# A row-sum kernel: early first loads, a 126+2 row layout with a split store, and a last row in three pieces

## The chip, the cores and the metric

The kernel runs on one core of one Trainium2 chip. Its engines are DVE (VectorE), ACT (ScalarE), POOL (GpSimd), PE (TensorE, unused here) and SP (SyncE, which issues the DMA transfers of this kernel; SPq is its queue). A transfer is issued by SP, is carried out as packets by 16 DMA engines, and ends with 16 completions (semaphore increments); its landing is the last of these. The metric is the device time of one execution in microseconds (us). A kernel is run several times; the text quotes medians. Ratios are the mean time of one kernel's fast runs over that of the other's fast runs of the same rounds on the same chip, so they are not quite the ratio of the medians quoted. The profile's span is some 1.8 us shorter than the device time of the same execution (162.6 and 164.42 us for the kernel before). The profiled execution of the kernel before is 0.4 us above its median.

## The reference

```python
def setup_inputs():
    batch, seq, dim = 32, 512, 1024
    return {"x": np.random.randn(batch, seq, dim).astype(np.float32), "divisor": float(dim)}

def reference(x, divisor):
    return (np.sum(x, axis=-1) / divisor).astype(np.float32)
```

So 16,384 rows of 1024 float32 (67.1 MB) are read, and 16,384 results (64 KB) are written.

## The kernel before

Partition p of 128 gets the 128 consecutive rows from 128p on. The rows come in nine bulk loads (14 rows per partition, the last one 8), then loads of 4, 2 and 1 rows, then the last row in two pieces. DVE (`reduce_sum`) and ACT (an activation that also sums) share the rows of each load. All results stand in one tile `res` of 128 x 128, which one store writes at the end: 512 B per partition, 512 B apart.

```python
    xr = x.tensor.reshape((P, J, D)).ap()          # P = 128 partitions, J = 128 rows each, D = 1024
    out_v = out.tensor.reshape((P, J)).ap()
    bulk = [14] * 7 + [14, 8]; tail = [4, 2]
    # ... three buffers of 14 rows; sums() splits each load between ACT and DVE ...
    c = 704
    t = one.tile([P, D], F32, name="row")          # the row before the last: one load, two sums
    # ... ACT sums t[:, c:], DVE sums t[:, :c], DVE combines and scales; DVE scales res[:, :126] ...
    t = one.tile([P, D], F32, name="last")         # the last row: two loads
    tc.keep_in_program_order(nc.sync.dma_start(out=t[:, :c], in_=xr[:, j, :c]))
    tc.keep_in_program_order(nc.sync.dma_start(out=t[:, c:], in_=xr[:, j, c:]))
    act_sum(part[:, 2:3], t[:, :c])
    nc.vector.reduce_sum(out=part[:, 3:4], in_=t[:, c:], axis=AX)
    nc.vector.tensor_scalar(out=res[:, j : j + 1], in0=part[:, 3:4], scalar1=part[:, 2:3],
                            scalar2=scale, op0=ADD, op1=MULT)
    tc.keep_in_program_order(nc.sync.dma_start(out=out_v, in_=res))
```

## Time and profile before

| What | Value | Read from |
|---|---|---|
| device time | 163.96 us (163.89 to 164.11) | three runs |
| DVE, ACT busy | 49%, 38% of the span | the page, part 1 |
| one DMA packet of 57,344 B | 2.116 us, so 27.1 GB/s on one of 16 engines, 434 GB/s on all | the trace's packets |
| first load issued, first load packet | 0.73 us, 1.74 us | timeline, packets |
| last load packet ends, last load's completion | 158.90 us, 159.35 us | packets, completion increments |
| last store issued, completed, span's end | 160.22, 161.77, 162.6 us | timeline, completion increments |

The first lines of the page show that the loads are the bound: neither compute engine is half busy, while DMA is at nine tenths in nearly every slice.

```profile
span 162.6 us, 213 instructions
DVE 79.3 (49%) x16; ACT 61.1 (38%) x115; POOL 0.2 (0%) x4
DMA  6999999989999999899999999999999999998990
GB/s 226 451 451 451 451 437 395 437 353 409 451 451 451 451 451 437 381 423 395 423 423 451 451 453 451 451 451 437 409 409 423 409 423 423 443 435 383 423 373 22
```

What can be saved lies at the two ends. The waits of SP's queue (who waited, for whom, us in total, times, longest) show at one end the opening barrier and at the other the completion of the store:

```profile
SPq L108 <- PEq L108: 0.7, 1, 0.7
SPq L122 <- DMA out_dram<-res: 1.0, 1, 1.0
```

The timeline of the start and of the end (start us, duration us, engine, line, operation) and the line of the store in the DMA view (count, KB, us from issue to landing):

```profile
0.73 1.33 SPq L61 DMA_DIRECT2D t<-in_x_dram  x3
...
159.03 0.76 ACT L50 ACTIVATE junk<-last 128x704 f32<-128x704 f32 x1 [0.32 <-DMA last<-in_x_dram]
159.27 0.21 DVE L76 TENSOR_SCALAR res<-part 128x1 f32<-128x1 f32 x1
159.40 0.47 DVE L87 TENSOR_REDUCE part<-last 128x1 f32<-128x320 f32 x1
159.98 0.21 DVE L88 TENSOR_SCALAR res<-part 128x1 f32<-128x1 f32 x1
160.22 0.35 SPq L91 DMA_DIRECT2D out_dram<-res  x1
```

```profile
out_dram<-res SPq DMA_DIRECT2D x1, 64.0 KB, 1.5
```

From the last landing (159.35) to the issue of the store (160.22) it takes 0.87 us, and from there to the landing of the store 1.55 us.

### The profile page before, as it was taken

The page shows a single profiled execution, that of the slowest core. Times are in us where ns is not written, and L with a number is a line of the kernel's source. Part 1 is how long each engine was busy: PE and PEld are TensorE (multiplying, and loading weights), DVE is VectorE, ACT ScalarE, POOL GpSimd, SP SyncE. Part 2 cuts the span into 40 slices and gives each one's busy share as a digit, 9 for nine tenths or more (in the row PEclk, how much of TensorE's full clock was granted, in tenths as well). Part 3 has the DMA queues.
Part 4 walks back from the last instruction along what each step waited for, and adds up shares of the span by engine and source line. Part 5 has one row for each costly group of instructions (what it writes and reads, how often), then busy time and mean ns, then how long its engine had stood idle before and what let it go on. Part 6 is the DMA issues. An engine that isn't in the chain of part 4 may idle for free.

```text
span 162.6 us, 213 instructions
## 1 busy us (share of the span) xinstructions
DVE 79.3 (49%) x16; ACT 61.1 (38%) x115; POOL 0.2 (0%) x4
## 2 busy tenths in 40 slices
DVE  0000099207940596039801990099108930697893
ACT  3000096006800490029201940095007700692882
POOL 0000000000000000000000000000000000000000
DMA  6999999989999999899999999999999999998990
GB/s 226 451 451 451 451 437 395 437 353 409 451 451 451 451 451 437 381 423 395 423 423 451 451 453 451 451 451 437 409 409 423 409 423 423 443 435 383 423 373 22
DMA packets 2161, 67.18 MB, mean 413 GB/s; under 512 B 240, under 2 KB 496, under 8 KB 752
## 3 DMA queue, kind: packets, MB, share of 16 engines
q1 hardware_dynamic: 2160, 67.18, 96.5%
q14 instruction: 1, 0.01, 0.0%
HBM read 67.11 MB, written 0.07 MB: 413 GB/s over the span
## 4 chain that ended last, share of the span: by engine, by line
DMA 74%; DVE 18%; another core or an unknown queue 5%; SPq 1%; issue 0%; DVEq 0%
DMA t<-in_x_dram 48%; DMA tail<-in_x_dram 25%; DVE res L56 17%; DVE part L75 0%; SPq L61 0%; SPq L66 0%; DVE part L87 0%; DVE res L79 0%; DVE res L88 0%; DVE res L76 0%; DVEq L88 0%; DVEq L76 0%; DVEq L79 0%
## 5 line engine op out<-in xcount | busy, mean ns | idle before, releaser
L56 DVE TENSOR_REDUCE res<-t 128x8 f32<-128x8192 f32 (+1 forms) x9 | 73.9, 8212 | 79.9 <-DMA t<-in_x_dram 79.9
L50 ACT ACTIVATE junk<-t 128x1024 f32<-128x1024 f32 x52 | 52.5, 1009 | 96.7 <-DMA t<-in_x_dram 96.7
L50 ACT ACTIVATION_READ_ACCUMULATOR junk<-t 128x1 f32 x52 | 9.7, 186 | 0.0
L56 DVE TENSOR_REDUCE res<-tail 128x2 f32<-128x2048 f32 (+1 forms) x2 | 3.5, 1753 | 0.7 <-DMA tail<-in_x_dram 0.7
L50 ACT ACTIVATE junk<-tail 128x1024 f32<-128x1024 f32 x3 | 3.1, 1022 | 0.9 <-DMA tail<-in_x_dram 0.9
L50 ACT ACT_TABLE_LOAD x1 | 1.3, 1283 | 0.7 <-PEq L108 0.7
L50 ACT ACTIVATE junk<-last 128x704 f32<-128x704 f32 x1 | 0.8, 761 | 0.3 <-DMA last<-in_x_dram 0.3
L75 DVE TENSOR_REDUCE part<-row 128x1 f32<-128x704 f32 x1 | 0.9, 880 | 0.0
L50 ACT ACTIVATION_READ_ACCUMULATOR junk<-tail 128x1 f32 x3 | 0.6, 186 | 0.0
L50 ACT ACTIVATE junk<-row 128x320 f32<-128x320 f32 x1 | 0.4, 441 | 0.1
L87 DVE TENSOR_REDUCE part<-last 128x1 f32<-128x320 f32 x1 | 0.5, 475 | 0.0
L79 DVE TENSOR_SCALAR res<-res 128x126 f32<-128x126 f32 x1 | 0.2, 228 | 0.1
L88 DVE TENSOR_SCALAR res<-part 128x1 f32<-128x1 f32 x1 | 0.2, 214 | 0.1
L76 DVE TENSOR_SCALAR res<-part 128x1 f32<-128x1 f32 x1 | 0.2, 214 | 0.1
L50 ACT ACTIVATION_READ_ACCUMULATOR junk<-last 128x1 f32 x1 | 0.2, 187 | 0.0
L50 ACT ACTIVATION_READ_ACCUMULATOR junk<-row 128x1 f32 x1 | 0.2, 186 | 0.0
L108 POOL MEMSET const-bfloat16-1.0<- 128x1 bf16 x1 | 0.1, 101 | 0.0
L108 POOL MEMSET const-uint8-127<- 128x1 uint8 x1 | 0.1, 101 | 0.0
L108 POOL MEMSET const-float32-0.0<- 128x1 f32 x1 | 0.1, 98 | 0.2 <-issue 0.2
L108 POOL MEMSET const-float32-1.0<- 128x1 f32 x1 | 0.1, 98 | 0.0
## 6 DMA issues: line engine op xcount, KB each, us to landing
t<-in_x_dram SPq DMA_DIRECT2D x8, 7168.0 KB, 42.1
t<-in_x_dram SPq DMA_DIRECT2D x1, 4096.0 KB, 34.8
tail<-in_x_dram SPq DMA_DIRECT2D x1, 2048.0 KB, 39.3
tail<-in_x_dram SPq DMA_DIRECT2D x1, 1024.0 KB, 41.4
row<-in_x_dram SPq DMA_DIRECT2D x1, 512.0 KB, 42.2
last<-in_x_dram SPq DMA_DIRECT2D x1, 352.0 KB, 42.6
last<-in_x_dram SPq DMA_DIRECT2D x1, 160.0 KB, 42.5
out_dram<-res SPq DMA_DIRECT2D x1, 64.0 KB, 1.5
```

The costliest lines, as they stand in the source:

```text
L50: nc.scalar.activation(junk[:, :n], src, COPY, accum_out=dst)
L56: nc.vector.reduce_sum(out=res[:, j : j + d], in_=t[:, :d, :], axis=AX)
L75: nc.vector.reduce_sum(out=part[:, 1:2], in_=t[:, :c], axis=AX)
L76: nc.vector.tensor_scalar(out=res[:, j : j + 1], in0=part[:, 1:2], scalar1=part[:, 0:1], scalar2=scale, op0=ADD, op1=MULT)
L79: nc.vector.tensor_scalar_mul(out=res[:, :j], in0=res[:, :j], scalar1=scale)
L87: nc.vector.reduce_sum(out=part[:, 3:4], in_=t[:, c:], axis=AX)
L88: nc.vector.tensor_scalar(out=res[:, j : j + 1], in0=part[:, 3:4], scalar1=part[:, 2:3], scalar2=scale, op0=ADD, op1=MULT)
L108: nc = _bacc.Bacc("TRN2", target_bir_lowering=False, num_devices=1)
```

## The change

Three things change at once. (1) The first three loads, which wait for nothing, move ahead of the program's opening barrier. (2) The rows are laid out in two regions: partition p takes 126 consecutive rows of the first 16,128 rows, and 2 consecutive rows of the last 256. The 126 results per partition can leave early in a store of their own, and the last store carries only 8 B per partition (1 KB in all, side by side in memory). (3) The last row comes in three pieces, and the scaling moves partly to POOL and ACT.

```diff
+def start_loads_at_once(nc):
+    sp = mybir.EngineType.SP
+    first, body = nc.main_func.blocks[0], nc.main_func.blocks[1]
+    # ... SP's leading DMAs without a wait are taken out of `body` ...
+    first.instructions = first.instructions[:at] + loads + first.instructions[at:]   # ahead of SP's drain
 ...
+    nc.at_finalize(start_loads_at_once)
-    xr = x.tensor.reshape((P, J, D)).ap()
-    out_v = out.tensor.reshape((P, J)).ap()
+    L = 2
+    M = J - L
+    x_main = bass.AP(tensor=x.tensor, offset=0, ap=[[M * D, P], [D, M], [1, D]])
+    x_last = bass.AP(tensor=x.tensor, offset=P * M * D, ap=[[L * D, P], [D, L], [1, D]])
+    o_main = bass.AP(tensor=out.tensor, offset=0, ap=[[M, P], [1, M]])
+    o_last = bass.AP(tensor=out.tensor, offset=P * M, ap=[[L, P], [1, L]])
 ...
-    # last row: load [:704], load [704:], ACT and DVE sum, DVE combines, one store of res
+    c = 768
+    act_sum(r[:, 0:1], row[:, c:], by=scale)
+    nc.vector.reduce_sum(out=q[:, 0:1], in_=row[:, :c], axis=AX)
+    a, b = 512, 768
+    load(pa, x_last[:, 1, :a])
+    load(pb, x_last[:, 1, a:b])
+    load(pc[:, : D - b], x_last[:, 1, b:])
+    nc.gpsimd.tensor_scalar_mul(out=res, in0=res, scalar1=scale)
+    tc.keep_in_program_order(nc.sync.dma_start(out=o_main, in_=res))
+    act_sum(pc[:, D - b : D - b + 1], pa)
+    nc.vector.reduce_sum(out=pc[:, D - b + 1 :], in_=pb, axis=AX)
+    nc.vector.reduce_sum(out=q[:, 1:2], in_=pc, axis=AX)
+    nc.vector.scalar_tensor_tensor(out=fin, in0=q, scalar=scale, in1=r, op0=MULT, op1=ADD)
+    tc.keep_in_program_order(nc.sync.dma_start(out=o_last, in_=fin))
```

More of the change, by code (lines that the diff above doesn't have):

```diff
@@ L12 @@
 AX = mybir.AxisListType.X
+def start_loads_at_once(nc):
+    sp = mybir.EngineType.SP
+    first, body = nc.main_func.blocks[0], nc.main_func.blocks[1]
+    loads = []
+    for i in body.instructions:
+        if i.engine == sp:
+            if type(i).__name__ != "InstDMACopy" or (i.sync_info and i.sync_info.on_wait):
+                break
+            loads.append(i)
+    names = {i.name for i in loads}
+    assert names
+    body.instructions = [i for i in body.instructions if i.name not in names]
+    at = next(
+        k for k, i in enumerate(first.instructions) if i.engine == sp and type(i).__name__ == "InstDrain"
+    )
+    first.instructions = first.instructions[:at] + loads + first.instructions[at:]
 @with_exitstack
@@ L29 @@
     assert J * P == N
-    xr = x.tensor.reshape((P, J, D)).ap()
-    out_v = out.tensor.reshape((P, J)).ap()
-    bulk = [14] * 7 + [14, 8]
+    L = 2
[4 more added lines that the diff above has]
+    o_last = bass.AP(tensor=out.tensor, offset=P * M, ap=[[L, P], [1, L]])
     split = {14: 6, 8: 4, 4: 2, 2: 1}
-    tail = [4, 2]
@@ L39 @@
-    assert sum(bulk) + sum(tail) + 2 == J
-    pool = ctx.enter_context(tc.tile_pool(name="bulk", bufs=3))
+    loads = [14] * 8 + [8, 4, 2]
+    assert sum(loads) == M
+    bulk = ctx.enter_context(tc.tile_pool(name="bulk", bufs=3))
     one = ctx.enter_context(tc.tile_pool(name="one", bufs=1))
     psum = ctx.enter_context(tc.tile_pool(name="junk", bufs=4, space=bass.MemoryType.PSUM))
-    res = one.tile([P, J], F32, name="res")
-    part = one.tile([P, 4], F32, name="part")
-    def act_sum(dst, src):
+    res = one.tile([P, M], F32, name="res")
@@ L48, in act_sum, with load @@
+    fin = one.tile([P, L], F32, name="fin")
+    q = one.tile([P, L], F32, name="q")
+    r = one.tile([P, L], F32, name="r")
+    nc.gpsimd.memset(r, 0.0)
+    def load(dst, src):
+        tc.keep_in_program_order(nc.sync.dma_start(out=dst, in_=src))
+    def act_sum(dst, src, by=1.0):
         n = src.shape[-1]
         junk = psum.tile([P, D], F32, name="junk")
-        nc.scalar.activation(junk[:, :n], src, COPY, accum_out=dst)
-    def sums(t, j, rows):
+        nc.scalar.activation(junk[:, :n], src, COPY, scale=by, accum_out=dst)
@@ L53, in sums @@
+    j = 0
+    for rows in loads:
+        if rows >= 8:
+            t = bulk.tile([P, 14, D], F32, name="t")
+        else:
+            t = one.tile([P, rows, D], F32, name=f"t{rows}")
+        load(t[:, :rows, :], x_main[:, j : j + rows, :])
         d = rows - split[rows]
-        for r in range(d, rows):
-            act_sum(res[:, j + r : j + r + 1], t[:, r, :])
+        for i in range(d, rows):
+            act_sum(res[:, j + i : j + i + 1], t[:, i, :])
         nc.vector.reduce_sum(out=res[:, j : j + d], in_=t[:, :d, :], axis=AX)
-    j = 0
@@ L59 @@
-    for i, rows in enumerate(bulk):
-        t = pool.tile([P, 14, D], F32, name="t")
-        tc.keep_in_program_order(nc.sync.dma_start(out=t[:, :rows, :], in_=xr[:, j : j + rows, :]))
-        sums(t, j, rows)
-        j += rows
-    for i, rows in enumerate(tail):
-        t = one.tile([P, rows, D], F32, name=f"tail{i}")
-        tc.keep_in_program_order(nc.sync.dma_start(out=t, in_=xr[:, j : j + rows, :]))
-        sums(t, j, rows)
-        j += rows
-    c = 704
-    t = one.tile([P, D], F32, name="row")
@@ L73 @@
-    tc.keep_in_program_order(nc.sync.dma_start(out=t, in_=xr[:, j, :]))
-    act_sum(part[:, 0:1], t[:, c:])
-    nc.vector.reduce_sum(out=part[:, 1:2], in_=t[:, :c], axis=AX)
-    nc.vector.tensor_scalar(
-        out=res[:, j : j + 1], in0=part[:, 1:2], scalar1=part[:, 0:1], scalar2=scale, op0=ADD, op1=MULT
-    )
-    nc.vector.tensor_scalar_mul(out=res[:, :j], in0=res[:, :j], scalar1=scale)
-    j += 1
-    t = one.tile([P, D], F32, name="last")
-    tc.keep_in_program_order(nc.sync.dma_start(out=t[:, :c], in_=xr[:, j, :c]))
@@ L85 @@
-    tc.keep_in_program_order(nc.sync.dma_start(out=t[:, c:], in_=xr[:, j, c:]))
-    act_sum(part[:, 2:3], t[:, :c])
-    nc.vector.reduce_sum(out=part[:, 3:4], in_=t[:, c:], axis=AX)
-    nc.vector.tensor_scalar(
-        out=res[:, j : j + 1], in0=part[:, 3:4], scalar1=part[:, 2:3], scalar2=scale, op0=ADD, op1=MULT
-    )
-    tc.keep_in_program_order(nc.sync.dma_start(out=out_v, in_=res))
+        j += rows
+    c = 768
+    row = one.tile([P, D], F32, name="row")
+    load(row, x_last[:, 0, :])
@@ new lines @@
+    act_sum(r[:, 0:1], row[:, c:], by=scale)
+    nc.vector.reduce_sum(out=q[:, 0:1], in_=row[:, :c], axis=AX)
+    a, b = 512, 768
+    pa = one.tile([P, a], F32, name="pa")
+    pb = one.tile([P, b - a], F32, name="pb")
+    pc = one.tile([P, D - b + 2], F32, name="pc")
+    load(pa, x_last[:, 1, :a])
[3 more added lines that the diff above has]
+    tc.keep_in_program_order(nc.sync.dma_start(out=o_main, in_=res))
```

## The prediction

> **What bounds the kernel.** The loads. In the DMA view 67.11 MB are read; the 14-row packets (57,344 B) take 2.116 us each, 27.1 GB/s on one of 16 engines, 434 GB/s together. The Trainium skill ("DMA: Bandwidth & Descriptors", Specifications) gives 435 GB/s as the fabric ceiling; the trace agrees. The engines have no gaps: the first load packet starts 1.74 us after the span's start, the last ends at 158.90, and the packets at their median durations alone need 155.2 us. DVE (49%) and ACT (38%) mostly wait for loads. So only the two ends can give anything: the head (first issue at 0.73 us, first packet 1.0 us later) and the tail (from the last landing at 159.35 us to the end at 162.6).
>
> **Head.** The waits view shows SP waiting 0.7 us for the opening barrier. With the loads ahead of it, the first issue moves from 0.73 to about 0.05 us, and the saturated stream moves with it: -0.65 to -0.7 us, all on the critical path. The barrier then ends later (three issues of about 0.4 us), which delays ACT's table load to about 2 us; the first data come at 19 us, so that costs nothing.
>
> **Layout.** Per partition the bulk loads are the same runs of 56 KB; only the distance between partitions changes, from 512 to 504 KB. Since the packets already run at the ceiling, I expect no change of the rate (within 0.3 us either way; this is the part I know least).
>
> **Tail, after the shift of 0.7 us.** The last row in pieces of 512, 256 and 256 columns costs about 0.06 us more DMA time than 704 and 320 (128 more packets of some 8 ns overhead, from 1280 B = 55 ns and 2816 B = 113 ns). The last piece lands at about 158.75 us. DVE: row piece of 768 columns to 158.35, second piece 158.4 to 158.8 (256 columns, an estimate of 0.41 us from 704 = 0.88 and 320 = 0.475), last reduction (258 columns, 0.41 us) about 158.9 to 159.3, final operation 0.21 us plus 0.1 us, so the store is issued at about 159.65 instead of 160.22: -0.55 us. From last landing to issue it takes 0.9 us against 0.87 before, so this restructuring by itself is about neutral: it replaces ACT's 704 columns after the last but one landing by one more DVE step. The 126 columns leave early (POOL scaling, off the path; issue near 158), hidden behind the final computation.
>
> **Last store.** 64 KB in 512 B packets (27 ns each, 8 per engine) becomes 8 B per partition; packets of about 10 ns (the semaphore writes of 4 B take 9) would save 0.14 us. The skill says that below 512 B the DMA does read-modify-write (same section); no run here shows its cost, so I count -0.1 us with 0.4 us of risk. Issue to landing was 1.5 us and is mostly latency, which stays.
>
> **Sum.** -0.7 (head) + 0.06 (pieces) + 0.05 (chain) - 0.1 (store) = -0.7 us: 163.96 becomes 163.2 us, range 162.5 to 163.8. That is 0.4%, so within 2%.
>
> **Right or wrong, what shows it.** First DMA issue near 0 and first packet near 1.0 us (head); median 14-row packet still 2.116 us and 16.9 us between bulk reductions (layout); last landing about 158.7; DVE's last operation ends about 159.65; last store's issue to landing 1.4 to 1.5 us.
>
> **What would make it wrong.** The timed span starting with the issue, so that the head gains nothing; a slower first issue; the 504 KB stride changing HBM behaviour, for better (the first packets of each engine took 2.5 to 3.0 us) or worse; 8-byte writes with a slow receipt; the main store or POOL blocking SP's queue before the last store.

## The result, and the profile after

The changed kernel takes 165.05 us (164.85 to 165.28, four runs) against 164.04 us for the kernel before on the same chip: ratio 1.0061, 95% interval 1.0042 to 1.0079. It was forecast to be 0.7 to 0.8 us faster (163.2 against 163.96) and is 1.0 us slower.

The same lines of the changed kernel: the timeline of the start and of the end, then its stores in the DMA view, then the waits of SP's queue.

```profile
0.00 1.34 SPq L76 DMA_DIRECT2D t<-in_x_dram  x3
...
157.92 0.35 SPq L115 DMA_DIRECT2D out_dram<-res  x1
157.99 0.60 ACT L81 ACTIVATE junk<-pa 128x512 f32<-128x512 f32 x1
158.27 0.42 DVE L118 TENSOR_REDUCE pc<-pb 128x1 f32<-128x256 f32 x1
158.52 0.19 ACT L81 ACTIVATION_READ_ACCUMULATOR junk<-pa 128x1 f32 x1
158.79 0.42 DVE L119 TENSOR_REDUCE q<-pc 128x1 f32<-128x258 f32 x1
159.31 0.16 DVE L120 SCALAR_TENSOR_TENSOR fin<-q,r 128x2 f32<-128x2 f32 x1
159.50 0.34 SPq L121 DMA_DIRECT2D out_dram<-fin  x1
```

```profile
out_dram<-res SPq DMA_DIRECT2D x1, 63.0 KB, 2.1
out_dram<-fin SPq DMA_DIRECT2D x1, 1.0 KB, 2.8
```

```profile
SPq L138 <- PEq L138: 0.2, 1, 0.2
SPq L152 <- DMA out_dram<-fin: 2.4, 1, 2.4
```

Up to the issue of the last store, all went as forecast: the loads start at 0.00 us instead of 0.73, the last landing is at 158.59 us (159.35 before), and the last store is issued at 159.50 us, 0.72 us earlier than before. Then the store of 1 KB takes 2.84 us from issue to landing where the store of 64 KB took 1.55. The wait for it at the end of the program grew from 1.0 to 2.4 us. So the two traces put the loss in this one store: -0.72 us at its issue, +1.29 us in its flight and +0.05 us from its landing to the end of the span (0.88 us before, 0.93 after) are +0.6 us, the difference of the two spans (162.65 and 163.27).

Its packets show where in its flight. Before, the 512 B packets ended at 161.42 us, and the 16 completions came between 161.59 and 161.77. After, the 8 B packets ended at 160.54 us (each took 9 ns), and the completions came between 160.75 and 162.34, scattered over 1.6 us. By these records the data had left quickly; the time went between the last packet and the last completion.

### The profile page after: what moved, and what is told of

It is laid out like the page before. It is cut to its first block, busy times and chain, and to the rows that moved or that the text cites. A ratio compares the mean times of both kernels' runs of the same rounds, so it can differ in the third digit from the quotient of the medians.

```text
span 163.3 us, 220 instructions
## 1 busy us (share of the span) xinstructions
DVE 79.4 (49%) x15; ACT 60.9 (37%) x115; POOL 0.8 (1%) x6
## 4 chain that ended last, share of the span: by engine, by line
DMA 74%; DVE 17%; another core or an unknown queue 5%; SPq 2%; issue 0%; DVEq 0%
DMA t<-in_x_dram 48%; DMA pb<-in_x_dram 26%; DVE res L93 16%; SPq L76 2%; DVE q L119 0%; DVE pc L118 0%; DVE fin L120 0%; DVEq L119 0%; DVEq L120 0%
## 5 line engine op out<-in xcount | busy, mean ns | idle before, releaser
L93 DVE TENSOR_REDUCE res<-t 128x8 f32<-128x8192 f32 (+3 forms) x11 | 77.4, 7038 | 79.8 <-DMA t<-in_x_dram 79.8
L81 ACT ACTIVATE junk<-t 128x1024 f32<-128x1024 f32 x55 | 55.5, 1010 | 95.8 <-DMA t<-in_x_dram 95.8
L81 ACT ACTIVATION_READ_ACCUMULATOR junk<-t 128x1 f32 x55 | 10.3, 187 | 0.0
L114 POOL TENSOR_SCALAR res<-res 128x126 f32<-128x126 f32 x1 | 0.5, 535 | 155.5 <-DVE res L93 155.5
L101 DVE TENSOR_REDUCE q<-row 128x1 f32<-128x768 f32 x1 | 1.0, 953 | 0.1
L81 ACT ACTIVATE junk<-pa 128x512 f32<-128x512 f32 x1 | 0.6, 601 | 0.1
```

The lines of the kernel that those rows point to most:

```text
L81: nc.scalar.activation(junk[:, :n], src, COPY, scale=by, accum_out=dst)
L93: nc.vector.reduce_sum(out=res[:, j : j + d], in_=t[:, :d, :], axis=AX)
L101: nc.vector.reduce_sum(out=q[:, 0:1], in_=row[:, :c], axis=AX)
L114: nc.gpsimd.tensor_scalar_mul(out=res, in0=res, scalar1=scale)
```

## The experiments

### First round: which part of the change loses the time?

My theory was that the head gained what was forecast and that the last store lost more. Two explanations of the small store were open. Theory A: a write of less than 512 B is completed slowly, whatever its neighbours. Theory B: 128 small writes into the same 1 KB get in each other's way. Rivals of both: the early start, or the three pieces, disturb the end of the program. All four kernels ran on one chip in five rounds, with the kernel before at 164.19 us.

**hoist_only**: the kernel before, with `start_loads_at_once` and nothing else.

```diff
+    nc.at_finalize(start_loads_at_once)
```

> The kernel before with only the first three loads ahead of the opening barrier. My theory (the head gains what was predicted, the last store loses more): first issue near 0, first packet near 1.0 us, everything after it 0.65 to 0.75 us earlier, last store issue to landing 1.5 us as before, so about 0.7 us (0.4%) faster than the kernel before, near 163.3 us. Rival (the early start gains nothing in the timed span, or is lost later in the stream): the same time as before, 163.9 to 164.2 us.

Measured: 163.43 us, 0.76 us below the kernel before (ratio 0.9954, interval 0.9941 to 0.9968). First packet 1.00 us, last landing 158.33 us, and the store as before:

```profile
0.00 1.32 SPq L83 DMA_DIRECT2D t<-in_x_dram  x3
...
159.22 0.35 SPq L113 DMA_DIRECT2D out_dram<-res  x1
```

```profile
out_dram<-res SPq DMA_DIRECT2D x1, 64.0 KB, 1.5
```

The head of the prediction holds; the early start alone gives a better kernel than either of the two.

**no_hoist**: the changed kernel without that line.

```diff
-    nc.at_finalize(start_loads_at_once)
```

> The changed kernel with its loads behind the barrier again. If head and tail simply add up: about 0.7 us slower than the changed kernel, 165.7 us, with the last store still taking about 2.8 us from issue to landing. Rival (starting early is what disturbs the end of the program): the last store falls back to 1.5 us and the time to about 164.4 us.

Measured: 165.62 us (ratio 1.0089, interval 1.0076 to 1.0103); the last store still takes 2.75 us from issue to landing (the view rounds it to 2.7):

```profile
out_dram<-fin SPq DMA_DIRECT2D x1, 1.0 KB, 2.7
```

The early start does not cause the slow store. From the two ratios, the early start is worth 0.0028, or 0.5 us, in the changed kernel; the two ran in different rounds, and their intervals allow the 0.76 us seen above. In the two traces the last store is issued 0.70 us earlier with the early start (159.50 and 160.20).

**aligned_split**: the changed kernel with the 128-row layout. The two stores stay, but the 8 B per partition now go to places 512 B apart.

```diff
-    x_main = bass.AP(...); x_last = bass.AP(...); o_main = bass.AP(...); o_last = bass.AP(...)
+    xr = x.tensor.reshape((P, J, D)).ap()
+    out_v = out.tensor.reshape((P, J)).ap()
+    x_main, x_last = xr[:, :M, :], xr[:, M:, :]
+    o_main, o_last = out_v[:, :M], out_v[:, M:]
```

> The changed kernel with its 128-row layout back, but still two stores: the last one writes 8 bytes per partition, now 512 B apart and no longer side by side in 1 KB. Theory A (a write of under 512 B is completed slowly whatever its neighbours): the last store takes 2.4 to 3.2 us from issue to landing, time 164.7 to 165.4 us. Theory B (128 small writes into the same 1 KB get in each other's way): the last store takes 1.4 to 1.7 us, time 163.3 to 163.8 us.

Measured: 163.54 us (ratio 0.9961, interval 0.9948 to 0.9973). The same 8 B per partition now take 1.42 us:

```profile
out_dram<-res SPq DMA_DIRECT2D x1, 63.0 KB, 1.5
out_dram<-fin SPq DMA_DIRECT2D x1, 1.0 KB, 1.4
```

Theory A falls: pieces of 8 B are as small here as in the changed kernel.

**one_store**: the 128-row layout and one store of `res`, as before; early loads and three pieces kept.

```diff
-    nc.gpsimd.tensor_scalar_mul(out=res, in0=res, scalar1=scale)
-    tc.keep_in_program_order(nc.sync.dma_start(out=o_main, in_=res))
+    nc.gpsimd.tensor_scalar_mul(out=res[:, :M], in0=res[:, :M], scalar1=scale)
 ...
-    nc.vector.scalar_tensor_tensor(out=fin, in0=q, scalar=scale, in1=r, op0=MULT, op1=ADD)
-    tc.keep_in_program_order(nc.sync.dma_start(out=o_last, in_=fin))
+    nc.vector.scalar_tensor_tensor(out=res[:, M:], in0=q, scalar=scale, in1=r, op0=MULT, op1=ADD)
+    tc.keep_in_program_order(nc.sync.dma_start(out=out_v, in_=res))
```

> The changed kernel with the 128-row layout and a single last store of 512 B per partition; three last pieces and early loads kept. Both theories of the small store: it takes 1.5 us from issue to landing, and is issued near 159.5 us of the span as in the changed kernel, so 163.4 us, about 1.5 us faster than the changed kernel. Rival (the extra time comes from the three pieces or from the early start, not from the store): stays above 164.5 us.

Measured: 163.64 us (ratio 0.9969, interval 0.9956 to 0.9981), store issued at 159.48 us and landed 1.55 us later. So the three pieces are no loss of 1 us; beside hoist_only (163.43) they gain nothing either, and 0.2 us more is within the two intervals.

### Second round: is it the neighbourhood of the writes, and what in it?

aligned_split changed the layout of the loads, too. **packed_only** takes that away: it is aligned_split but for the destination of the last store. Its result is wrong.

```diff
-    o_main, o_last = out_v[:, :M], out_v[:, M:]
+    o_main = out_v[:, :M]
+    o_last = bass.AP(tensor=out.tensor, offset=P * M, ap=[[L, P], [1, L]])
```

> The 128-row layout of aligned_split for all loads and for the main store; only the last store's 128 pieces of 8 bytes go side by side into one 1 KB (so the result is wrong, on purpose). Theory B (neighbouring small writes get in each other's way): last store 2.4 to 3.1 us from issue to landing, about 1.3 us slower than aligned_split, near 164.9 us. Rival (the 126+2 layout of the loads, or the main store of 504 B runs, is what slows the end): 1.4 us and 163.5 us as aligned_split.

Measured: 165.06 us (ratio 1.0046, interval 1.0034 to 1.0059). In its trace:

```profile
out_dram<-res SPq DMA_DIRECT2D x1, 63.0 KB, 1.5
out_dram<-fin SPq DMA_DIRECT2D x1, 1.0 KB, 3.2
```

The two edits differ in the addresses of 128 writes and in nothing else, and the ratios (each against the kernel before on its own chip) differ by 0.0085, or 1.4 us. One thing comes with the addresses: the 1 KB lies inside what the main store writes, so here the last store also waits for the main store. That costs nothing: the main store landed at 159.25 us and DVE's last sum ended at 159.29. The changed kernel has no such overlap and is slow too. This settles the cause: the 8 B pieces side by side. The layout of the loads and the main store is not it.

**widths** adds 15 stores to the end of the kernel before, each issued after the landing of the one before it, with the pieces' width and spacing varied. A full store at the end makes the result right.

```diff
+    def again(name, w, step):
+        s = one.tile([P, w], F32, name=name)
+        nc.vector.tensor_copy(out=s, in_=res[:, :w])
+        to = bass.AP(tensor=out.tensor, offset=0, ap=[[step, P], [1, w]])
+        tc.keep_in_program_order(nc.sync.dma_start(out=to, in_=s))
+        nc.vector.memset(s, 0.0)
+    again("w2s2", 2, 2); again("w2s4", 2, 4)   # ... and so on; w and step in elements of 4 B
```

> The kernel before, then 15 further stores, one after the other, each on an idle queue: 8 bytes per partition at a spacing of 8, 16, 32, 64, 128, 256 and 512 bytes, then 64 B and 256 B side by side, 64 B at 512 B, 504 B side by side and at 512 B, and repeats of 8 B. Theory B: from issue to landing 2.5 to 3 us at a spacing of 8 B, falling to 1.4 us at a spacing that is the size of the shared block (64 B is my guess, so slow at 8, 16 and 32, fast from 64 or 128 on); 64 B and 256 B side by side fast; 504 B side by side somewhat slow (about 2 us, as pieces share blocks at their ends), 504 B at 512 B fast. Theory A (size alone) is already against aligned_split: it would make every store here but the 512 B one slow. The total time is not compared.

Measured, from issue to landing: 8 B at a spacing of 8 B took 2.83 us and on repetition 2.90 us; at 16, 32, 64, 128, 256 and 512 B it took 1.39 to 1.50 us. Pieces of 64 B and 256 B side by side took 1.41 and 1.44 us, and 504 B 1.55 us side by side and 1.52 at 512 B. The direction of theory B holds, but my guess that 16 B and 32 B would also be slow was a miss in this run.

**spacings** repeats part of this forwards and backwards with further patterns (`run16B`: pieces of 16 B side by side; `gap16B`: 8 B every 16 B; `eng4KB`: groups of eight 8 B pieces 32 B apart, the groups 4 KB apart; x marks the second pass). That each group falls to one DMA engine, as the expectations here and in the next run have it, is an assumption: the traces do not show which engine writes which piece. I forgot the full store at the end, so its result is wrong; the stores' times are not touched by that. Each store still waited for the one before.

```diff
+    again("gap8B", 2, [[2, P]], 0); again("run4B", 1, [[1, P]], 0)
+    again("eng4KB", 2, [[1024, 16], [8, 8]], 0)   # ... nine patterns, then the same backwards
```

> The kernel before, then 18 stores on an idle queue to a region written just before: nine patterns, then the same nine backwards. The width probe had 8 B at a spacing of 8 B slow (2.8 to 2.9 us) and 8 B at 16 B fast (1.4 us). If the spacing of 8 B is what is slow and order does not matter: gap8B 2.8 us in both passes, gap16B 1.4 us in both. If what counts is how many pieces fall into one block of 64 B: run4B slow as gap8B or slower, run16B and run32B (each piece beside the next, 4 and 2 to a block) 1.4 us. The eng patterns put an engine's eight 8 B pieces 32 B apart and vary the distance between engines: 4 KB was slow; if the distance matters, 512 B is near 1.4 us and the time grows towards 4 KB; if the form of the pattern (two steps) is what is slow, all four are alike.

Its DMA view (last column: us from issue to landing):

```profile
out_dram<-gap8B SPq DMA_DIRECT2D x1, 1.0 KB, 3.0
out_dram<-gap16B SPq DMA_DIRECT2D x1, 1.0 KB, 1.7
out_dram<-run4B SPq DMA_DIRECT2D x1, 0.5 KB, 7.4
out_dram<-run16B SPq DMA_DIRECT2D x1, 2.0 KB, 2.7
out_dram<-run32B SPq DMA_DIRECT2D x1, 4.0 KB, 1.4
...
out_dram<-eng4KB SPq DMA_DIRECT2D x1, 1.0 KB, 3.8
...
out_dram<-run32Bx SPq DMA_DIRECT2D x1, 4.0 KB, 1.4
out_dram<-run16Bx SPq DMA_DIRECT2D x1, 2.0 KB, 1.4
out_dram<-run4Bx SPq DMA_DIRECT2D x1, 0.5 KB, 7.5
out_dram<-gap16Bx SPq DMA_DIRECT2D x1, 1.0 KB, 2.5
out_dram<-gap8Bx SPq DMA_DIRECT2D x1, 1.0 KB, 3.1
```

For pieces that follow each other evenly, crowding goes with the time: 4 B side by side 7.4 and 7.5 us, 8 B 3.0 and 3.1 us, 32 B 1.4 us both times. At four pieces to 64 B the time varies between passes and runs: 1.4 or 2.7 us for 16 B side by side, 1.4 to 2.5 us for 8 B at 16 B. A second effect shows that crowding in 64 B is not the whole story: 8 B at a spacing of 32 B takes 1.4 us when it runs on evenly over 4 KB (the width probe), but with the groups 512 B, 1 KB, 2 KB and 4 KB apart 2.2, 1.8, 2.8 and 3.8 us in the first pass and 1.8, 2.5, 2.6 and 3.7 us in the second. These two-step patterns also start their packets some 0.4 us later (1.2 instead of 0.83 us after the issue), which leaves little to explain at 512 B and some 2 us at 4 KB. So the distance between groups matters, as one of the expectations had it, and the form of the pattern is not all. What in the memory makes the writes wait for each other stays open.

**who_shares** asked whether a block shared between engines or an engine's own successive writes cost more.

```diff
+    again("own64", 2, [[1024, 16], [2, 8]])   # groups of eight pieces side by side, groups 4 KB apart
+    again("mix64", 2, [[2, 16], [32, 8]])     # the 1 KB of pack2, its pieces in another order
```

> The kernel before, then eight further stores, one after the other: 8 bytes per partition 512 B apart (far2), side by side (pack2, twice), and with the neighbours chosen: own64 and own256 put the eight pieces of one DMA engine side by side (8 B or 32 B apart) with engines 4 KB apart; mix64 and mix256 put pieces of 16 different engines side by side and the pieces of one engine 128 B or 512 B apart. If a block shared between engines is what costs: mix slow (2 us or more), own fast (1.4 us). If one engine's successive writes to one block queue up: own slow, mix fast. If both: both slow.

Measured: far2 1.41, pack2 2.82 and 3.47, own64 3.95, mix64 3.13, own256 4.30, mix256 1.78 us. This does not decide between the two accounts. own256, whose groups are also 4 KB apart but less crowded, is as slow as own64, so the distance alone may make own64 slow. mix64 fills the same 1 KB as pack2 in another order and takes as long, and mix256 has the addresses of the fast 32 B spacing of widths and is fast but for its later start. What these runs show is that the set of addresses goes with the time in these two pairs, whatever the order.

**fresh** asked whether memory that this execution had not yet written is slower.

```diff
+    again("newgap8B", 2, [[2, P]], 0)      # ... first stores to unwritten parts, before any full store
+    again("newrun504B", 126, [[126, P]], 0)
+    again("oldrun504B", 126, [[126, P]], 0)
```

> The kernel before with its store replaced by 11 stores on an idle queue, the first to parts of the result that this execution has not written yet, the later ones to parts already written, and a full store at the end. The changed kernel's 504 B store took 2.1 us in its place and 1.5 us in the width probe, where the region had just been written. If memory not written yet is what is slow: newrun504B about 2 us or more, oldrun504B 1.5 us, newgap16B and newgap32B above 1.4 us, oldgap16B 1.4 us. If it makes no difference: 504 B 1.5 us both times, 8 B at a spacing of 8 B 2.8 us both times, 8 B at 16 B 1.4 us both times.

The run is inconclusive for its first five stores and for its last two of 8 B: they go to disjoint places, so they did not wait for each other and overlapped. The 504 B store took 1.66 us the first time and 2.16 us the second, the wrong way round for the idea of fresh memory. In all runs with it side by side it took between 1.5 and 2.4 us, and 512 B apart 1.5 us in every run; why it varies is open. In the changed kernel it lands at 159.98 us, before the last store's first packet at 160.34.

### Third: better versions

**fused_end** is aligned_split with the last reduction and scaling in one DVE operation.

```diff
-    act_sum(pc[:, D - b : D - b + 1], pa)
-    # ... reduce pb and pc, then scalar_tensor_tensor
+    act_sum(r[:, 1:2], pa, by=scale)
+    # ... DVE combines the row before the last, then reduces pb into pc[:, 256]
+    nc.vector.tensor_scalar(out=pd, in0=pc[:, : D - b + 1], scalar1=scale, scalar2=r[:, 1:2],
+                            op0=MULT, op1=ADD, accum_out=fin[:, 1:2])
```

> An attempt at a better kernel: aligned_split, with the last reduction and the final scaling in one DVE operation that starts its sum from ACT's scaled part. The final operation (0.16 us and 0.1 us before it) leaves the chain and a read of the accumulator comes in: last store issued 0.1 to 0.25 us earlier, 163.3 to 163.45 us against 163.54. If the fused operation is slower by more than it saves, no gain.

Measured: 163.42 us, ratio 0.9954 (0.9939 to 0.9968), not told apart from aligned_split (0.9961). From last landing (158.51) to issue (159.40) it takes 0.89 us, no less than in the kernel before: DVE was still busy with the pieces before.

**tuned_end** balances those pieces.

```diff
-    c = 768;  a, b = 512, 768
+    c = 640;  a, b = 512, 704
+    # and the combination of the row before the last runs on POOL
```

> fused_end with the ends of the two engines balanced: the row before the last is cut at 640 instead of 768 columns, the last row in 512, 192 and 320, and the combination for the row before the last runs on POOL, so that DVE is free when its pieces land. Last landing to issue of the last store about 0.65 to 0.75 us instead of 0.9, so 163.15 to 163.3 us, against 163.42 for fused_end and hoist_only. If the chain is not bound there, 163.4 us.

Measured: 163.29 us, ratio 0.9946 (0.9932 to 0.9959). Last landing 158.34, issue 159.12: 0.78 us instead of 0.89, not the 0.65 to 0.75 hoped for. The interval overlaps that of hoist_only.

**eight_rows** keeps the whole idea of the change, two regions and a last store side by side, but with 120+8 rows, so that the last store's pieces are 32 B.

```diff
-    L = 2
+    L = 8          # the loads of 4 and 2 rows now come from x_last, their sums go to fin
```

> The changed kernel with its idea kept (rows in two regions, split store, last store side by side) but 120+8 rows instead of 126+2, so that the last store's pieces are 32 B, two to each 64 B instead of eight. By the spacing probe (32 B side by side: 1.4 us in both passes; 8 B: 3.0 and 3.1 us) the last store takes 1.4 to 1.5 us from issue to landing and the kernel 163.4 to 163.7 us, like aligned_split. Rival (the layout of two regions, in loads or main store, has a cost of its own): above 164.2 us although the pieces are wider.

Measured: 163.22 us beside 164.05 us for the kernel before, ratio 0.9950 (0.9937 to 0.9963). That is faster than expected: its last load landed at 158.09 us, 0.5 us earlier than in the changed kernel, and no run isolates why. The main store waits behind the queued loads (5.1 us) and is complete before the last one is issued at 159.06 us; the last one is as fast as expected:

```profile
out_dram<-res SPq DMA_DIRECT2D x1, 60.0 KB, 5.1
out_dram<-fin SPq DMA_DIRECT2D x1, 4.0 KB, 1.4
```

A store four times as large takes half the time. All three of these, and hoist_only, beat the kernel before by some 0.5% (and the changed kernel by some 1%), and their intervals overlap; hoist_only gets it with the least code.

## Why the prediction was wrong

- **What bounds the kernel**: right. The packets' median is 2.116 us in both kernels, and the compute engines wait in both. The Trainium skill ("DMA: Bandwidth & Descriptors", Specifications) puts the fabric ceiling at 435 GB/s; the trace's packets make 434.
- **Head, -0.65 to -0.7 us**: right; hoist_only measured -0.76 us, and the first packet came at 1.02 us, as forecast.
- **Layout of the loads, no change of rate**: right. The packets' mean, which a median can hide, is 2.124 to 2.138 us in the traces with 128-row layout and 2.132 in those with two regions. The same skill page (Latency and other measured facts) reports copies between HBM tensors at a row pitch of 512 KiB at 207 GB/s, against 214 at a pitch of 4 MiB padded by 4 KiB. This kernel's loads show no such difference: 2.116 us per packet (median) at 512 KB and at 504 KB.
- **Tail, store issued at about 159.65 us and neutral by itself**: right to 0.15 us; it was issued at 159.50. From last landing to issue it took 0.91 us (0.9 forecast).
- **Last store, "I count -0.1 us with 0.4 us of risk"**: this is the step that failed. It measured +1.29 us in the trace, and 1.4 us in the comparison of packed_only with aligned_split. The term was mis-sized because I treated a small write as a matter of its width. The packets were indeed 9 ns each and ended early; the completions came late. Why such writes complete late stays open. The -0.1 us is what the same store gives 512 B apart (1.42 instead of 1.55 us). The skill's remark on read-modify-write below 512 B pointed at a cost, but the runs put it on the crowding of the pieces.
- Among what would make it wrong I had named "8-byte writes with a slow receipt", but gave it far too little weight: the range ended at 163.8 us.

The sum from the separate runs: -0.76 (head, hoist_only), +0.2 (three pieces, one_store against hoist_only), -0.1 (splitting the store, aligned_split against one_store), +1.4 (side by side, packed_only against aligned_split): +0.7 us. The two middle terms are not told apart from zero by their intervals. The measured ratio of 1.0061 is +1.0 us with an interval of 0.7 to 1.3 us.

## What to carry to other kernels

A store at the very end of a program is paid from issue to the last confirmation, so look at the landing of the last DMA and not at its bytes; a smaller last store can be slower. Where many partitions write to neighbouring places, try pieces of 32 B or more (32, 64 and 256 B took 1.4 us), or pieces evenly apart (8 B every 512 B was fast in each run); here that was worth 1.4 us. Distance alone is no guarantee: groups of 8 B pieces 4 KB apart were slow. Loads that wait for nothing can start ahead of the opening barrier, which gave this load-bound kernel the whole 0.7 us of that wait.

## What the Trainium skill lacked or had wrong

- "DMA: Bandwidth & Descriptors", Specifications: the line on transfers below 512 B gives a width for line rate and a read-modify-write below it, but nothing on how close the writes lie to each other. For the time of one store, width alone did not decide here: 8 B per partition took 1.42 us from issue to landing when 512 B apart and 2.7 to 3.2 us side by side in the kernels (up to 3.5 in a probe); 512 B took 1.55 us.
- No page that I read has the cost of crowded small writes: side by side, pieces of 4 B took 7.4 us, 8 B about 3 us, 16 B 1.4 or 2.7 us, 32, 64 and 256 B 1.4 us, and 8 B every 32 B in groups of eight 4 KB apart 3.7 to 4.3 us.
- "DMA: Bandwidth & Descriptors", Specifications, gives some 358 GB/s as the HBM limit of one core. The row lacks the condition that the page's section Bandwidth gives, both cores of the pair streaming. With one core running, this kernel read 413 GB/s on average over its span and 434 GB/s by its packets.
- No page that I read has the gain from issuing loads ahead of the opening barrier: 0.76 us here.
